# Layer 0 of a two-layer decoder trunk: one pair of K's columns in the place of V's second half behind the first projection, the input's statistics on two engines, V's second half behind the mixer's end

## The chip, the cores and the metric

The kernel runs on one core of a Trainium2 chip, as one program. The metric is the device time of one execution in microseconds (us), the median of the runs shown. The core has a tensor engine (PE) that writes matrix products into PSUM banks, a vector engine (DVE), a scalar engine (ACT), a third elementwise engine (POOL), and a queue engine (SP) that issues most transfers (DMA) between HBM and the core's memory SBUF.

## What is computed

Two post-norm layers over 512 tokens of width 1024, all in float32. The reference, cut to the parts that matter here:

```python
h = layer_norm(x, ln0_g, ln0_b)
for l in range(DEPTH):                      # DEPTH = 2
    mix = hybrid_mixer(h, w_in[l], ...)     # causal convolution (31 taps) + gated linear attention
    h = layer_norm(DEEPNORM_ALPHA * h + mix, ln1_g[l], ln1_b[l])
    xa = memory_cross_attention(h, mem, w_xq[l], w_xkv[l], w_xo[l])
    h = layer_norm(DEEPNORM_ALPHA * h + xa, ln2_g[l], ln2_b[l])
    ff = swiglu(h, w_ffn_in[l], w_ffn_out[l])
    h = layer_norm(DEEPNORM_ALPHA * h + ff, ln3_g[l], ln3_b[l])

def hybrid_mixer(h, w_in, ...):
    c_a, c_g, q, k, v, r, a_low = jnp.split(h @ w_in, cuts, axis=-1)
    u = causal_depthwise_conv(c_a * jax.nn.sigmoid(c_g), conv_w, conv_b)
    u = jax.nn.silu(layer_norm(u, conv_ln_g, conv_ln_b))
    ...
    o = rms_norm(gla_chunked(q, k, v, log_a), gla_norm_g) * jax.nn.silu(r)
    return jnp.concatenate([u, o], axis=-1) @ w_out

def memory_cross_attention(x, mem, w_q, w_kv, w_o):
    k, v = jnp.split(mem @ w_kv, 2, axis=-1)   # K and V need mem and weights only
    ...
```

K and V of the cross-attention (256 memory rows, 1024 columns each) depend on the memory and the weights alone. So their projections can stand anywhere ahead of the attention, and the kernel uses them as work for PE where PE would otherwise wait.

## The kernel before, in words

**Tiling.** Tokens lie in four tiles h0 to h3 of 128 rows. A projection is 128x128 weights against up to 512 moving columns. Each float32 operand is split into a high and a low part: ACT copies the high part (`hi`), DVE or POOL subtracts it from the source (`lo`), and `mm3` issues three matmuls (lines 170 to 172: high with high, high with low, low with high). A weight chunk of 512 KB comes through `wchunk`: a DMA by SP into one of 4 raw buffers, the high copy on ACT (line 161), the low part on the engine that `wlo_engines` named last (line 163), into one of 4 ring buffers. `split` (lines 111, 112) does the same to activations and evictions. The PSUM tag `acc` has four banks; `tr` and `cv` have two each.

**Order.** Each engine runs its own queue in order. The order is laid down when the program is built, by a scheduler that goes by estimated durations and priorities (`high_priority` brings forward, the convolution's taps have the lowest). `issue_after(x)` puts the instructions traced within it behind x, on x's engine alone.

**Front of layer 0.** `first_V` loads the memory, transposes it and computes V's first half (512 columns, 4 chunks, lines 163 to 172 on tiles pt_xv_first). Then the four x tiles are loaded. V's second half (pt_xv, again 4 chunks of weights, 48 matmuls of 512 columns) is worked between the steps of the first layer norm, and is written as a generator with pauses: first its first chunk, then after the statistics three of its parts, and its last part behind the transposes of k = 3. The statistics: `bn_stats` on DVE twice a tile (line 788) and `bn_aggr`, tile 3's behind the low part of V's first chunk; then a chain of ten small DVE instructions to y0 and b0 (lines 790 to 792); ACT normalises the four tiles (line 805); PE transposes 32 blocks (lt_ln, line 811); ACT scales each of eight k tiles (xf, line 813) and `split` makes hT. The first matmul of the mixer's projection (pp_c) needs hT's first tile and the first chunk of w_c.

**Mixer.** `conv_in` projects two halves to u, `conv_taps` runs 31 taps on each of four channel tiles on DVE (line 887, lowest priority), and gates, q, k, v and the state S of the linear attention (GLA) are worked beside them.

**Mixer's end, layer 0.** In the program's order: the first half of `conv_norm` (cn: transposes cvt, line 1009, statistics, chain to b at line 1015, evictions by ACT at line 1019); K's first pair of columns (`mem_K` with pr = 0: 256 columns, 2 chunks, 48 matmuls of 256 columns on pp_xk), its eviction behind that chain's end (end0); GLA's first pair with r's first group (pt_r), then r's second; the second half of cn (end1); K's pairs 1 to 3; the weights of the output projection (w_mo, 8 chunks, low parts behind end1); then the rest of cn and GLA's second pair. The output projection (po_mo) follows.

Of the kernel before, what the change touches and what calls it, by code (L numbers as in the profile page):

```python
# [51 lines left out]
def trunk(ctx: ExitStack, tc, a, out):  # L52
# [15 lines left out]
    def f(ap):  # L68
        return ap.bitcast(F32)
# [38 lines left out]


    def split(hi, lo, src, eng=DVE):  # L110
        ins = ACT.activation(hi, src, AF.Copy)  # L111
        eng.tensor_sub(lo, src, f(hi))  # L112
        return ins
# [19 lines left out]
    behind_act = []  # L133
    lo_end = [None]

# [33 lines left out]
    def mm3(o, lh, ll, rh, rl, start, stop):  # L169
        PE.matmul(o, lh, rh, start=start, stop=False)  # L170
        PE.matmul(o, lh, rl, start=False, stop=False)  # L171
        return PE.matmul(o, ll, rh, start=False, stop=stop)  # L172

# [78 lines left out]

    def proj_feat(w, mov, specs, name, n=T, halves=False, after=None):

        work = []
        for si, (c0, ncol, evac) in enumerate(specs):
            kk = 1024 // ncol
            wcs = [wchunk(w[ci * kk * P:(ci + 1) * kk * P, c0:c0 + ncol], kk, ncol, f"{name}{si}{ci}", after=after)
                   for ci in range(NK // kk)]
            banks = [bank(f"pp_{name}{si}{m}") for m in range(ncol // P)]  # L260
            work.append((kk, wcs, banks, evac))
        parts = [(0, n // 2), (n // 2, n)] if halves else [(0, n)]
        for t0, t1 in parts:
            for kk, wcs, banks, evac in work:
# [12 lines left out]

    def proj_tok(w, mov, c0, evac, name, groups=((0, 1), (2, 3)), after=None, pause=False):

        wcs = []

        def chunk(ci):
            wcs.append(wchunk(w[ci * 2 * P:(ci + 1) * 2 * P, c0:c0 + 512], 2, 512, f"{name}{ci}",
                              after=after if ci else None))

        for ci in range(1 if pause else 4):
            chunk(ci)
        if pause:  # L290
            yield
            for ci in (1, 2):
                chunk(ci)
        for grp in groups:
            banks = {tt: bank(f"pt_{name}_{tt}") for tt in grp}
            for ci in range(4):
                if pause and ci == 3:
                    yield
                    chunk(3)
                    yield  # L300
                wh, wl = wcs[ci]
# [391 lines left out]

    def mem_K(l, mT, KT, pr, after=None, evict_after=None):
# [4 lines left out]
        proj_feat(a["w_xkv"][l], mT, [(pr * 256, 256, evac)], f"xk{pr}_{l}", n=MEM, after=after)  # L699

    def new_V(l):
        return [block([P, 2, D], F32R, f"V{j}_{l}") for j in range(2)]

    def mem_V(l, mT, V, c, **kw):
        cs = slice(c * 512, (c + 1) * 512)
        return proj_tok(a["w_xkv"][l], mT, D + c * 512,
                     lambda mt, ps: split(V[0][:, mt, cs], V[1][:, mt, cs], ps), f"xv{c}_{l}", groups=((0, 1),), **kw)

# [11 lines left out]
    def first_V():  # L720
# [48 lines left out]
        return end, lo_end[0], evict  # L769

    V0_end, lo0_end, V0_evict = first_V()
    load_x(0, 1, 2, 3)
    nc.sync.dma_start(lnrow[0:NK, :], a["ln0_g"].rearrange("(k p) -> k p", p=P))
    nc.sync.dma_start(lnrow[NK:2 * NK, :], a["ln0_b"].rearrange("(k p) -> k p", p=P))
    KT = new_K(0)
    hT = new_hT("ln0")
    V1 = mem_V(0, mT, V, 1, pause=True)
    next(V1)
    V1_lo = lo_end[0]
    with tc.high_priority(offset=HP):  # L780
# [9 lines left out]
        DVE.tensor_scalar(v0, mv0[:, :, 1], EPS, VS, ALU.add, ALU.mult)  # L790
        y0 = rstd_of(v0, NT, "ln0")
        chain_end = DVE.scalar_tensor_tensor(b0, mv0[:, :, 0], -1.0, y0, ALU.mult, ALU.mult)
# [8 lines left out]
    with tc.issue_after(chain_end.ins):  # L801
        DVE.tensor_copy(lncol, pl[:, :2 * NK])
    with tc.high_priority(offset=HP):
        for tt in range(NT):
            normed = ACT.activation(h[tt], h[tt], AF.Identity, scale=y0[:, tt:tt + 1], bias=b0[:, tt:tt + 1])
        with tc.issue_after(normed.ins):
            next(V1)
        for k in range(NK):
            pt = bank(f"lt_ln0_{k}", tag=("tr", "cv")[k % 2])
            for tt in range(NT):  # L810
                turned = PE.transpose(pt[:, tt * P:(tt + 1) * P], h[tt][:, k * P:(k + 1) * P], ident)
            xf = tmp.tile([P, T], F32, tag="t", name=f"xf{k}")
            xf_ins = ACT.activation(xf, pt, AF.Identity, scale=lncol[:, k:k + 1], bias=lncol[:, NK + k:NK + k + 1])
# [21 lines left out]
    for l in range(L):  # L835
# [272 lines left out]
        if l > 0:  # L1108
# [156 lines left out]
```

## Time and profile before

| | |
|---|---|
| median of 3 runs | 1404.52 us (1404.28 to 1404.99) |
| profiled execution | 1405.92 us, span 1404.2 us |
| PE busy | 1379.3 us, 98% of the span |
| PE weight loads busy | 1235.1 us, 88% |
| DVE busy | 1076.7 us, 77% |
| ACT busy | 672.5 us, 48% |
| POOL busy | 160.3 us, 11% |
| HBM traffic | 163 GB/s over the span |

The span is one execution as the profiler saw it, the time adds what lies around it. An instruction's row gives its start, its duration, the engine, the line, what it writes and reads, and in brackets how long its engine had been idle and what ended that. Matmuls overlap: a row of 0.39 us can start every 0.23 us, so prices are taken from start to start. PEclk is the granted clock of PE as a share of full speed. "x" is a count of merged instructions.

### The profile page before, as it was taken

The page shows a single profiled execution, that of the slowest core. Times are in us where ns is not written, and L with a number is a line of the kernel's source. Part 1 is how long each engine was busy: PE and PEld are TensorE (multiplying, and loading weights), DVE is VectorE, ACT ScalarE, POOL GpSimd, SP SyncE. Part 2 cuts the span into 40 slices and gives each one's busy share as a digit, 9 for nine tenths or more (in the row PEclk, how much of TensorE's full clock was granted, in tenths as well). Part 3 has the DMA queues.
Part 4 walks back from the last instruction along what each step waited for, and adds up shares of the span by engine and source line. Part 5 has one row for each costly group of instructions (what it writes and reads, how often), then busy time and mean ns, then how long its engine had stood idle before and what let it go on. Part 6 is the DMA issues. An engine that isn't in the chain of part 4 may idle for free.

```text
span 1404.2 us, 22523 instructions
## 1 busy us (share of the span) xinstructions
PE 1379.3 (98%) x8847; PEld 1235.1 (88%) x8847; DVE 1076.7 (77%) x1901; ACT 672.5 (48%) x1108; POOL 160.3 (11%) x123
## 2 busy tenths in 40 slices
PE   8999799999999999999999999999999999999997
PEld 6788598988899899989897889889889998998996
DVE  6589885756888878877668999675569886878766
ACT  5663271343466456545345235624435653664551
POOL 0384001110000000001014200011100000000000
PEclk9999999999999999999999999999999999999998
DMA  6444166695255665565334234669814646646641
GB/s 250 147 131 138 32 193 168 197 270 163 76 135 150 195 176 144 167 191 135 122 99 161 64 116 166 232 156 264 204 61 123 179 143 190 178 136 200 160 136 60
DMA packets 131230, 217.95 MB, mean 155 GB/s; under 512 B 8988, under 2 KB 83440, under 8 KB 130612
## 3 DMA queue, kind: packets, MB, share of 16 engines
q1 hardware_dynamic: 118132, 176.40, 38.1%
q0 software_dynamic: 12704, 39.85, 14.7%
q8 instruction: 69, 1.13, 0.3%
q14 instruction: 37, 0.30, 0.1%
q10 hardware_dynamic: 288, 0.26, 0.1%
HBM read 191.32 MB, written 37.75 MB: 163 GB/s over the span
## 4 chain that ended last, share of the span: by engine, by line
PE 86%; DVE 8%; DMA 2%; ACT 2%; issue 1%; SPq 0%; DVEq 0%; ACTq 0%; POOLq 0%
PE fx L600 5%; PE fx L602 5%; PE fx L601 5%; DVE cv L887 4%; PE fw L602 3%; PE fw L601 3%; PE fw L600 3%; PE pp_xq L171 2%; PE pp_xq L170 2%; PE pp_xq L172 2%; PE po_xo L172 2%; PE po_xo L171 2%; PE po_xo L170 2%; PE po_mo L170 2%; PE po_mo L171 2%; PE po_mo L172 2%
## 5 line engine op out<-in xcount | busy, mean ns | idle before, releaser
L887 DVE SCALAR_TENSOR_TENSOR cv<-u,chan,cv 128x511 f32<-128x511 f32 (+29 forms) x240 | 159.8, 731 | 0.2
L112 DVE TENSOR_TENSOR w_s<-s,w_s 128x1024 fp32r<-128x1024 f32 x80 | 97.6, 1220 | 33.8 <-ACT w_s L111 33.3
L111 ACT ACTIVATE w_s<-s 128x1024 fp32r<-128x1024 f32 x80 | 84.4, 1056 | 63.6 <-DMA s<-raw_a 37.1
L355 POOL DMA_DIRECT2D s<-raw_a x40 | 34.8, 881 | 625.1 <-PE pp_f L172 142.6
L600 PE MATMUL fx<-T_ln,w_s 128*128 128x256 f32 x320 | 90.6, 284 | 0.0
L602 PE MATMUL fx<-T_ln,w_s 128*128 128x256 f32 x320 | 90.5, 283 | 0.0
L601 PE MATMUL fx<-T_ln,w_s 128*128 128x256 f32 x320 | 90.5, 283 | 0.0
L111 ACT ACTIVATE w_a<-raw_a 128x1024 fp32r<-128x1024 f32 x60 | 63.1, 1056 | 32.1 <-issue 10.5
L112 DVE TENSOR_TENSOR w_a<-raw_a,w_a 128x1024 fp32r<-128x1024 f32 x60 | 73.2, 1220 | 4.7 <-ACT w_a L111 4.3
L222 ACT ACTIVATE junk<-h,nm_ln 128x1024 uint8<-128x1024 f32 x18 | 20.7, 1150 | 103.3 <-DVE nm_ln L221 100.9
L600 PEld LDWEIGHTS fx<-T_ln,w_s 128*128 128x128 f32 x320 | 61.4, 192 | 0.3 <-ACT u L613 0.2
L601 PEld LDWEIGHTS fx<-T_ln,w_s 128*128 128x128 f32 x320 | 61.4, 192 | 0.0
L602 PEld LDWEIGHTS fx<-T_ln,w_s 128*128 128x128 f32 x320 | 61.4, 192 | 0.0
L171 PE MATMUL pp_xq<-hT_ln,w_xq 128*128 128x256 f32 (+1 forms) x192 | 61.0, 321 | 0.0
L170 PE MATMUL pp_xq<-hT_ln,w_xq 128*128 128x256 f32 (+1 forms) x192 | 60.2, 321 | 0.5 <-ACT hT_ln L111 0.5
L172 PE MATMUL pp_xq<-hT_ln,w_xq 128*128 128x256 f32 (+1 forms) x192 | 60.1, 319 | 0.0
L171 PE MATMUL pp_c<-hT_ln,w_c 128*128 128x512 f32 (+1 forms) x160 | 55.3, 348 | 0.2 <-DVE hT_ln L112 0.2
L172 PE MATMUL pp_c<-hT_ln,w_c 128*128 128x512 f32 (+1 forms) x160 | 55.2, 348 | 0.0
L170 PE MATMUL pp_c<-hT_ln,w_c 128*128 128x512 f32 (+1 forms) x160 | 53.9, 349 | 0.7 <-DVE h L344 0.5
L355 POOL DMA_DIRECT2D S_fs<-w_ffn_out x16 | 17.2, 1073 | 313.9 <-DMA S_fs<-w_ffn_out 252.2
L111 ACT ACTIVATE w_S_fo<-raw_S_fo 128x1024 fp32r<-128x1024 f32 x32 | 33.8, 1058 | 36.0 <-PE foX_fo L563 14.2
L171 PE MATMUL po_xo<-w_xo,oTh 128*128 128x512 f32 x128 | 49.8, 392 | 0.0
(399 smaller groups left out, 4858.1 us busy)
## 6 DMA issues: line engine op xcount, KB each, us to landing
raw_a<-w_ffn_in SPq DMA_DIRECT2D x60, 512.0 KB, 3.7
s<-raw_a POOLq DMA_DIRECT2D x40, 512.0 KB, 5.5
raw_fo<-w_ffn_out SPq DMA_DIRECT2D x36, 512.0 KB, 3.4
S_fs<-w_ffn_out SPq DMA_DIRECT2D x32, 512.0 KB, 7.5
raw_S_fo<-S_fs SPq DMA_DIRECT2D x32, 512.0 KB, 4.4
s<-w_ffn_in SPq DMA_DIRECT2D x20, 512.0 KB, 5.4
raw_c<-w_in SPq DMA_DIRECT2D x16, 512.0 KB, 4.8
raw_xk<-w_xkv SPq DMA_DIRECT2D x16, 512.0 KB, 3.5
```

Source lines behind the costliest of these rows:

```text
L111: ins = ACT.activation(hi, src, AF.Copy)
L112: eng.tensor_sub(lo, src, f(hi))
L170: PE.matmul(o, lh, rh, start=start, stop=False)
L171: PE.matmul(o, lh, rl, start=False, stop=False)
L172: return PE.matmul(o, ll, rh, start=False, stop=stop)
L222: ACT.activation(junk, ht, AF.Square, bias=nm, accum_out=v)
L355: POOL.dma_start(dst, src, accum_op=ALU.add, max_dma_last_dim=4096)
L600: PE.matmul(o, wh, bh, start=start and k == 0, stop=False, skip_group_check=True)
L601: PE.matmul(o, wh, bl, start=False, stop=False, skip_group_check=True)
L602: PE.matmul(o, wl, bh, start=False, stop=stop and k == 3, skip_group_check=True)
L887: DVE.scalar_tensor_tensor(cv[ct][:, s:], u[:, ct, :T - s], wj, cv[ct][:, s:], ALU.mult, ALU.add)
```

## The change

In the front, V's second half is gone; in its place the first pair of K's columns is worked, in two steps (its first chunk, and after the statistics' chain the rest). x's first tile is loaded ahead of V's last chunk, and its statistics go behind a memory split on DVE. Tile 1's statistics are made on ACT as two sums, tiles 2 and 3 on DVE behind the low part of V's last chunk; the low part of V's third chunk goes to POOL. K's first chunk is split behind the statistics of tile 3, and the chain behind that split. The transposes go behind K's last matmul. Tiles 1 and 3 are normalised on DVE, and xf of k = 3, 5 and 7 is made there. At the mixer's end K's pair 1 comes first and is evicted without a tie, r is finished before cn starts, and the order is then GLA's first pair, K's pair 2, cn's second half, K's pair 3, V's second half (its DVE work behind end1), w_mo. Layer 1 keeps its order.

```diff
 def first_V():
+        turned_lo = lo_end[0]
+        wlo_engines(POOL)
         chunk(2, copied)
+        wlo_engines(DVE)
         mem_load(1, 1)
+        load_x(0)
+        with tc.issue_after(turned_lo.ins):
+            stats(0)
         with tc.issue_after(turned.ins):
             turned, copied = turn_after(work(1, 0), 1, 1)
         chunk(3, copied)
...
+    def stats_act(tt):
+        with tc.high_priority(offset=HP):
+            sm = small.tile([P, 2], F32, tag="sums", name=f"sums_ln0{tt}")
+            nm = small.tile([P, 1], F32, tag="nm", name=f"nm_ln0{tt}")
+            ACT.activation(junk, h[tt], AF.Copy, accum_out=sm[:, 0:1])
+            DVE.tensor_scalar(nm, sm[:, 0:1], -1.0 / D, None, ALU.mult)
+            ACT.activation(junk, h[tt], AF.Square, bias=nm, accum_out=sm[:, 1:2])
+            DVE.tensor_scalar(mv0[:, tt, :], sm, 1.0 / D, None, ALU.mult)
...
-    load_x(0, 1, 2, 3)
+    load_x(1, 2, 3)
...
-    V1 = mem_V(0, mT, V, 1, pause=True)
-    next(V1)
-    V1_lo = lo_end[0]
+    stats_act(1)
+    with tc.issue_after(lo0_end.ins):
+        stats(2)
+        st3 = stats(3)
+    K0_pause = mem_K(0, mT, KT, 0, parts=True)
+    with tc.issue_after(st3.ins):
+        next(K0_pause)
+    first_lo = lo_end[0]
     with tc.high_priority(offset=HP):
-        for tt in range(NT):
...
+        with tc.issue_after(first_lo.ins):
+            DVE.tensor_scalar(v0, mv0[:, :, 1], EPS, VS, ALU.add, ALU.mult)
         y0 = rstd_of(v0, NT, "ln0")
         chain_end = DVE.scalar_tensor_tensor(b0, mv0[:, :, 0], -1.0, y0, ALU.mult, ALU.mult)
-    with tc.issue_after(chain_end.ins):
+    with tc.issue_after(chain_end.ins), tc.issue_after(V0_end.ins):
+        next(K0_pause)
+        run(K0_pause)
         V0_evict()
-    with tc.issue_after(chain_end.ins), tc.issue_after(V0_end.ins):
-        next(V1)
+    K0_end = mm_end[0]
...
-    with tc.high_priority(offset=HP):
+    with tc.high_priority(offset=HP), tc.issue_after(K0_end.ins):
         for tt in range(NT):
-            normed = ACT.activation(h[tt], h[tt], AF.Identity, scale=y0[:, tt:tt + 1], bias=b0[:, tt:tt + 1])
-        with tc.issue_after(normed.ins):
-            next(V1)
+            if tt % 2:
+                DVE.tensor_scalar(h[tt], h[tt], y0[:, tt:tt + 1], b0[:, tt:tt + 1], ALU.mult, ALU.add)
+            else:
+                ACT.activation(h[tt], h[tt], AF.Identity, scale=y0[:, tt:tt + 1], bias=b0[:, tt:tt + 1])
...
+            if k in (3, 5, 7):
+                DVE.tensor_scalar(xf, pt, g_, b_, ALU.mult, ALU.add)
+            else:
+                xf_ins = ACT.activation(xf, pt, AF.Identity, scale=g_, bias=b_)
             split(hT[0][k // 4][:, k % 4, :], hT[1][k // 4][:, k % 4, :], xf)
-            if k == 3:
-                with tc.issue_after(turned.ins), tc.issue_after(xf_ins.ins):
-                    run(V1)
...
 # the mixer's end, layer 0
-            with tc.high_priority(offset=HP):
-                end0, took0 = next(cn)
-            mem_K(l, mT, KT, 0, evict_after=end0)
+            mem_K(l, mT, KT, 1)
             gla = gla_pair(0)
             next(gla)
+            run(proj_r)
+            r_end = mm_end[0]
+            wlo_engines(DVE)
+            with tc.high_priority(offset=HP), tc.issue_after(r_end.ins):
+                end0, took0 = next(cn)
             with later(end0):
                 run(gla)
-            run(proj_r)
-            wlo_engines(DVE)
+            mem_K(l, mT, KT, 2)
             with tc.high_priority(offset=HP):
                 end1, took1 = next(cn)
-            for pr in range(1, 4):
-                mem_K(l, mT, KT, pr, after=end0 if pr > 1 else None, evict_after=end1 if pr > 1 else end0)
+            mem_K(l, mT, KT, 3, after=end0)
+            with later(end1):
+                mem_V(l, mT, V, 1)
```

More of the change, by code (lines that the diff above doesn't have):

```diff
@@ L133, in trunk @@
     behind_act = []
-    lo_end = [None]
     def behind(load):
@@ L171, in mm3 @@
         PE.matmul(o, lh, rl, start=False, stop=False)
-        return PE.matmul(o, ll, rh, start=False, stop=stop)
+        mm_end[0] = PE.matmul(o, ll, rh, start=False, stop=stop)
+        return mm_end[0]
     def rstd_of(v, n, name):
@@ L251, in layer_norm, with proj_feat, proj_feat_parts @@
             split(hT[0][i][:, :, ts_], hT[1][i][:, :, ts_], pv)
-    def proj_feat(w, mov, specs, name, n=T, halves=False, after=None):
+    def proj_feat(*args, **kw):
+        run(proj_feat_parts(*args, **kw))
+    def proj_feat_parts(w, mov, specs, name, n=T, halves=False, after=None, parts=False):
         work = []
@@ L257, in proj_feat @@
             kk = 1024 // ncol
-            wcs = [wchunk(w[ci * kk * P:(ci + 1) * kk * P, c0:c0 + ncol], kk, ncol, f"{name}{si}{ci}", after=after)
-                   for ci in range(NK // kk)]
+            wcs = []
+            for ci in range(NK // kk):
+                wcs.append(wchunk(w[ci * kk * P:(ci + 1) * kk * P, c0:c0 + ncol], kk, ncol, f"{name}{si}{ci}", after=after))
+                if parts:
+                    yield
             banks = [bank(f"pp_{name}{si}{m}") for m in range(ncol // P)]
             work.append((kk, wcs, banks, evac))
-        parts = [(0, n // 2), (n // 2, n)] if halves else [(0, n)]
-        for t0, t1 in parts:
+        for t0, t1 in [(0, n // 2), (n // 2, n)] if halves else [(0, n)]:
             for kk, wcs, banks, evac in work:
@@ L276, in proj_feat, with proj_tok @@
                             evac(m, bk[:, :n])
[L278 to L293, printed above, removed]
+    def proj_tok(w, mov, c0, evac, name, groups=((0, 1), (2, 3))):
+        wcs = [wchunk(w[ci * 2 * P:(ci + 1) * 2 * P, c0:c0 + 512], 2, 512, f"{name}{ci}") for ci in range(4)]
         for grp in groups:
             banks = {tt: bank(f"pt_{name}_{tt}") for tt in grp}
[L296 to L301, printed above, removed]
+            for ci, (wh, wl) in enumerate(wcs):
                 for tt in grp:
@@ L692, in later, with mem_K @@
         return tc.issue_after(ins.ins) if ins is not None else nullcontext()
-    def mem_K(l, mT, KT, pr, after=None, evict_after=None):
+    def mem_K(l, mT, KT, pr, after=None, evict_after=None, parts=False):
         def evac(m, ps):
@@ L697, in evac, with mem_V @@
                 split(KT[0][:, pr * 2 + m, :], KT[1][:, pr * 2 + m, :], ps)
-        proj_feat(a["w_xkv"][l], mT, [(pr * 256, 256, evac)], f"xk{pr}_{l}", n=MEM, after=after)
+        work = proj_feat_parts(a["w_xkv"][l], mT, [(pr * 256, 256, evac)], f"xk{pr}_{l}", n=MEM, after=after, parts=parts)
+        return work if parts else run(work)
     def new_V(l):
         return [block([P, 2, D], F32R, f"V{j}_{l}") for j in range(2)]
-    def mem_V(l, mT, V, c, **kw):
+    def mem_V(l, mT, V, c):
         cs = slice(c * 512, (c + 1) * 512)
-        return proj_tok(a["w_xkv"][l], mT, D + c * 512,
-                     lambda mt, ps: split(V[0][:, mt, cs], V[1][:, mt, cs], ps), f"xv{c}_{l}", groups=((0, 1),), **kw)
+        run(proj_tok(a["w_xkv"][l], mT, D + c * 512,
+                     lambda mt, ps: split(V[0][:, mt, cs], V[1][:, mt, cs], ps), f"xv{c}_{l}", groups=((0, 1),)))
     def load_x(*tts):
@@ L769, in first_V, with stats @@
         return end, lo_end[0], evict
+    mv0 = const.tile([P, NT, 2], F32, name="mv0")
+    v0 = const.tile([P, NT], F32, name="v0")
+    b0 = const.tile([P, NT], F32, name="b0")
+    def stats(tt):
+        with tc.high_priority(offset=HP):
+            st = ln_stats(tt, "ln0")
+            for i in range(2):
+                end = DVE.bn_stats(st[:, i, :], h[tt][:, i * 512:(i + 1) * 512])
+            DVE.bn_aggr(mv0[:, tt, :], st)
+        return end
+    def stats_act(tt):
+        with tc.high_priority(offset=HP):
+            sm = small.tile([P, 2], F32, tag="sums", name=f"sums_ln0{tt}")
[4 more added lines that the diff above has]
+            DVE.tensor_scalar(mv0[:, tt, :], sm, 1.0 / D, None, ALU.mult)
     V0_end, lo0_end, V0_evict = first_V()
-    load_x(0, 1, 2, 3)
+    load_x(1, 2, 3)
     nc.sync.dma_start(lnrow[0:NK, :], a["ln0_g"].rearrange("(k p) -> k p", p=P))
@@ L1115, in trunk @@
             for c in range(2):
-                run(mem_V(l, mT, V, c))
+                mem_V(l, mT, V, c)
             mo = []
```

16 lines of the change are left out of this document (4 added, 12 removed).

## The prediction

> **What bounds the kernel now.** I read the busy table of the page, then what the tensor engine (PE) waited for, then stretches around those waits, then the order in time there.
>
> ```profile
> span 1404.2 us, 22523 instructions
> ...
> PE 1379.3 (98%) x8847; PEld 1235.1 (88%) x8847; DVE 1076.7 (77%) x1901; ACT 672.5 (48%) x1108; POOL 160.3 (11%) x123
> ```
>
> ```profile
> PE pt_r L170 <- DVE KT L112: 3.8, 1, 3.8
> PE cvt L1009 <- ACT acc L889: 3.2, 2, 1.8
> PE lt_ln L811 <- ACT h L805: 1.7, 1, 1.7
> ...
> PE po L1065 <- DVE attT L1055: 1.3, 1, 1.3
> PE pt_xv L171 <- DVE w_xv L163: 1.0, 2, 0.5
> ```
>
> PE is the bound, so only PE time that is idle or at a slow clock can be won. The large waits stand at two places of layer 0: the front (lt_ln, pt_xv) and the mixer's end (pt_r, cvt, po).
>
> ```profile
> core 0: us, PE busy (x) PEld busy (x) DVE busy (x) ACT busy (x) POOL busy (x), PEclk, DMA share, GB/s
> 20.50:40.75 20.25, 17.25 (x83) 13.51 (x82) 12.99 (x26) 15.29 (x20) 0.00 (x0) 0.92 0.45 137
> 25.40:31.60 6.20, 4.04 (x12) 3.03 (x13) 4.55 (x9) 5.58 (x5) 0.00 (x0) 0.73 0.36 102
> 61.50:162.80 101.30, 98.02 (x550) 79.44 (x548) 96.47 (x158) 40.18 (x62) 56.98 (x24) 1.00 0.34 110
> 150.00:172.00 22.00, 13.77 (x106) 10.61 (x105) 19.50 (x54) 8.10 (x25) 0.00 (x0) 0.84 0.00 0
> 168.50:171.30 2.80, 2.78 (x7) 2.20 (x8) 2.41 (x13) 1.55 (x4) 0.00 (x0) 0.50 0.00 0
> 172.00:207.00 35.00, 35.00 (x298) 31.91 (x297) 25.92 (x47) 25.65 (x50) 0.00 (x0) 1.00 0.51 163
> ```
>
> Mixer's end, 150 to 172 us: 22.00 - 13.77 = 8.2 us idle, and 2.78 us of matmuls at clock 0.50, which lose 1.4 more: **9.6 us**. VectorE (DVE) is nearly full from 61.5 to 162.8 us (96.5 of 101.3): it runs the convolution's taps, and PE runs out of work before they end.
>
> ```profile
> 159.14 1.08 PE L1075 MATMUL po<-S,qk 64*64 64x128 f32 x12
> ...
> 159.32 3.50 DVE L887 SCALAR_TENSOR_TENSOR cv<-u,chan,cv 128x485 f32<-128x485 f32 x5
> ...
> 163.97 0.77 PE L1009 MATMUL cvt<-ident,acc 128*128 128x128 f32 x5 [1.39 <-ACT acc L889]
> ...
> 167.86 0.16 DVE L1015 SCALAR_TENSOR_TENSOR b<-mv,y_cln 128x2 f32<-128x2 f32 x1
> ...
> 168.52 0.80 PE L170 MATMUL pt_r<-w_r,hT_ln 128*128 128x512 f32 x1 [3.78 <-DVE KT L112]
> ...
> 175.07 1.03 PE L1009 MATMUL cvt<-ident,acc 128*128 128x128 f32 x8
> ...
> 182.50 0.39 PE L172 MATMUL pt_r<-w_r,hT_ln 128*128 128x512 f32 x1
> ...
> 183.75 0.16 DVE L1015 SCALAR_TENSOR_TENSOR b<-mv,y_cln 128x2 f32<-128x2 f32 x1
> ...
> 206.93 0.40 PE L170 MATMUL po_mo<-w_mo,cUh 128*128 128x512 f32 x1
> ```
>
> PE has used up its work at 160.2, the taps end at 162.8, and r's second half (pt_r) starts only at 168.5, because its PSUM banks are held by the first K columns, whose eviction is tied behind the first normalisation (b, 167.86).
>
> **The change part by part.** *Moves on PE.* Prices by start to start:
>
> ```profile
> 127.69 0.39 PE L171 MATMUL pt_v<-w_v,hT_ln 128*128 128x512 f32 x1
> ...
> 133.36 0.39 PE L172 MATMUL pt_v<-w_v,hT_ln 128*128 128x512 f32 x1
> ...
> 134.71 0.39 PE L170 MATMUL pp_xk<-mT,w_xk 128*128 128x256 f32 x1
> ...
> 140.57 0.40 PE L170 MATMUL pt_r<-w_r,hT_ln 128*128 128x512 f32 x1
> ```
>
> 5.67 us for 25 steps of 512 columns is 0.227 each; 5.86 us for 48 of 256 columns is 0.122 each. V's second half is 48 of the first, 10.9 us; one K pair 48 of the second, 5.9 us. The front loses 5.0 us of work, the mixer's end gains the same: in sum nothing. What counts is the idle time.
>
> *Front before.* From 20.50 to 40.75 PE has 10.9 us of V, and 32 transposes at 0.11 (eight took 1.03), 3.5 us; with 0.2 for the small one, 14.6 of 20.25. **5.6 us** are lost.
>
> *Front after.* What ends last before the transposes is the statistics, then the chain to b, then the normalised tiles:
>
> ```profile
> 19.97 1.06 ACT L161 ACTIVATE w_xv<-raw_xv 128x1024 fp32r<-128x1024 f32 x1 [4.62 <-DMA raw_xv<-w_xkv]
> ...
> 23.76 0.17 DVE L790 TENSOR_SCALAR v<-mv 128x4 f32<-128x4 f32 x1
> ...
> 25.55 0.16 DVE L792 SCALAR_TENSOR_TENSOR b<-mv,y_ln 128x4 f32<-128x4 f32 x1
> 25.75 4.64 ACT L805 ACTIVATE h<-h,b,y_ln 128x1024 f32<-128x1024 f32 x4 [1.86 <-DVE b L792]
> ...
> 40.75 0.71 PE L170 MATMUL pp_c<-hT_ln,w_c 128*128 128x512 f32 x2
> ```
>
> ```profile
> L163 DVE TENSOR_TENSOR w_xk<-raw_xk,w_xk 128x1024 fp32r<-128x1024 f32 x14 | 17.0, 1220 | 0.7 <-ACT w_xk L161 0.6
> ...
> L187 DVE TENSOR_SCALAR t_ln<-y_ln,v_ln 128x1 f32<-128x1 f32 x48 | 13.0, 271 | 1.0
> ...
> L1186 DVE TENSOR_SCALAR p<-p,ss 128x256 f32<-128x256 f32 x32 | 10.1, 357 | 0.5
> ...
> L193 DVE TENSOR_SCALAR y_ln<-t_ln,y_ln 128x1 f32<-128x1 f32 x24 | 5.1, 212 | 0.6
> ...
> L885 DVE TENSOR_SCALAR cv<-u,chan 128x512 f32<-128x512 f32 x8 | 6.4, 810 | 0.1
> ```
>
> The first weight chunk still comes by DMA at about 19.9: in SP's queue the same loads stand before it, with x's first tile moved ahead of V's last chunk. Its split takes 1.06 on ACT and 1.22 on DVE, to 22.2, and the chain (23.76 to 25.71, 2.0 us) now follows at once, since tiles 2 and 3 had their statistics before it and tile 1 on ACT, which waited 4.62 us there. The chain ends at 24.2, 1.5 us earlier. That DVE tile 0's statistics wait for x, and that V's third chunk is split on POOL at 2.4 instead of 1.2 us, I cost at nothing: V's first half is not what ends last; without that cover it would be some 1.2 us.
>
> Normalising: two tiles on ACT (2.3 us) beside two on DVE. DVE's price bounds from rows: 128x512 into PSUM took 810 ns, 539 above the two-scalar 128x1 form, so 1.05 ns an element and 1.35 us for 1024; 128x256 within SBUF took 357, 145 above the one-scalar form, 0.57 ns an element and 0.85 us. The h tiles lie in SBUF like the second, so I take 0.85; either way ACT's 2.3 us hides most of it. All four tiles are ready near 26.5 (before: 30.4). The Trainium skill (VectorE: DVE Perf Modes, Mode 2×_2P) says that a one-source fp32 operation wholly in SBUF runs at two elements a cycle; the two rows agree (0.57 against 1.05 ns), and by a rate of one a cycle the sum would be 0.5 us less won, 1397.5.
>
> K's second chunk is split behind the chain. Behind two tiles on DVE's queue it ends at 24.2 + 1.7 + 1.2 = 27.1, ahead of them at 25.4; eight matmuls wait for it, and behind K's last one stand all transposes. I take the later, some 28, for the first transpose. First projection matmul at about 30, not 40.75. By then PE has done 5.9 of K and 16 transposes (1.8) of 9.5: 1.8 us lost. From there ACT and DVE make hT:
>
> ```profile
> L813 ACT ACTIVATE xf<-lt_ln,lncol 128x512 f32<-128x512 f32 x8 | 6.0, 789 | 2.6 <-PE lt_ln L811 2.6
> L111 ACT ACTIVATE hT_ln<-xf 128x512 fp32r<-128x512 f32 x8 | 4.9, 648 | 0.0
> ```
>
> ACT: five xf and eight hi copies at some 0.7, and three weight splits of 1.06: 12 us to 41. DVE: eight lo at 0.69, three xf at 0.81, three to four weight splits, V's eviction 1.3: as much. One k tile each 1.5 us; PE needs 1.4 us for g's two banks on it, plus the transposes, so it about keeps pace; I add 1.3 us of starving, from nothing (PE paced by g, then a) to 4 (a's weights late). The clock: after a wait of 1.7 us and sparse work it was 0.73 over 25.40 to 31.60; I put 1.0 for that (0 to 1.7). Lost after: 1.8 + 1.3 + 1.0 = 4.1, **1.5 us won** (bounds: 2.5 lost, 4.5 won). The Trainium skill (TensorE: Matmul & The Clock Gate, Part 1) ties the half clock to an idle window of about 3.4 us. By it the short gaps would cost no clock, the front would win 2.5, and the time would be 1396.0; this trace shows 0.73 after a wait of 1.7 us, so I keep my 1.0.
>
> *Transfers.* SP issues two chunks of 512 KB instead of four in the front (the two weight chunks and x in order, so the projection's first chunk comes no later than before, nearer 22 than 32, if a raw buffer is free); at the mixer's end it issues four of V ahead of w_mo's eight, two of K fewer. There the DMA engines were busy at 0.51, 163 GB/s; 1 MB more is 6 us of that rate beside 35 us, and V's tie on DVE comes later than its data: nothing, unless the four raw buffers hold w_mo's loads behind V's splits (in the 8.4 below).
>
> *Mixer's end after.* K's second pair is evicted at once, so r's second half has banks and runs on: 10.9 us of work from the point where PE stood. It covers the 2.6 us to the taps' end, and PE reaches r's end some 8 us after it. K's eviction takes 0.8 us of DVE from the taps, covered by those 8. The normalisation's transposes are tied behind r; from their start (163.97) to b took 4.0 us, and K's third pair (5.9) hides it. Second round: before, 175.07 to 183.75 is 8.8 us, the chain's steps interleaved with weight splits on DVE's in-order queue. In that time PE has K's fourth pair (5.9, its low halves behind the first b) and V's half (10.9, low halves behind the second b, two thirds of its matmuls need only high halves). From r's end PE then has 5.9 + 5.9 + 10.9, and transposes and GLA: 24.2 before from 182.7 to 206.9, less three K pairs, 6.6, and two rounds of transposes and GLA's (2.7) that stood earlier; 32 us in all. DVE's additional work here is four V splits (4.9) and V's eviction (1.3), less two K splits (2.4) and one K eviction (0.8), which come earlier: 3.0 us, against 9.1 idle in 172 to 207; ACT adds four V splits and an eviction less the same of K, 2.5 us, against 9.4. It fits, but narrowly between the second b and w_mo, where DVE's queue is in order and w_mo's splits stand behind V's. I keep the 1.3 us of attT and take 2.2 us of new waits (0 to 8.4: PE through with the third pair 7.6 us after r's end, and the fourth pair's splits only behind a second b at 16). Lost after 3.5, **6.1 us won** (0 to 9.6).
>
> Sum: 7.6 us. The profiled execution took 1405.92 us (span 1404.2, 1.7 around it), 1.4 above the median of 1404.52; from that median the sum gives **1397.0 us**.
>
> **Rivals.** *Both places fill better:* no new wait at the end, front wins 3: 9.6 + 3.0 - 1.3 = 11.3, 1393. For it: hT can start 10 us earlier. Against: DVE and ACT are then both full in 30 to 41. *The hole moves:* r's second half is free, but PE then waits for the first b and splits, six or so of the 9.6 us return, front nothing: 3 us won, 1401.5. For it: the chain now starts after r, not after the taps. *DVE takes over the end (slower):* from the second b to w_mo DVE has to do K and V splits (7.3), four of w_mo (4.9), evictions (2.1), GLA's part and the convolution's low halves (11): 25 us; if b comes 16 us after r's end and DVE waits for ACT as in 172 to 207, w_mo starts 46 us after r's end instead of 32, 14 us lost for the 9.6, the front's 1.5 besides: 1407.4. It decides once DVE is more than 11 us late.
>
> **How the numbers follow.** Forecast (1394.5 to 1400) 0.55; fills better 0.20; hole moves (1400 to 1404) 0.14, of which 0.05 is faster by over 0.2% (2.8 us, about what a measurement of this kernel can tell from no change) and 0.09 within; slower rival 0.11, of which 0.02 within. Faster 0.80, same 0.11, slower 0.09. The range leaves out the slower rival, the edge of the hole and a quarter of the better case: 1391.5 to 1403.0; the forecast's own is 1394.5 to 1400.
>
> **What would show it.** Right: pt_r no longer waits for KT and its matmuls run gapless; the first pp_c near 30; b of the input near 24.2; no clock of 0.50 at 168 to 171. Wrong: waits of pt_xv or pp_xk on DVE splits above 3 us, po_mo on w_mo, or pp_c on hT above 3.

## The result and the profile after

| | before | changed |
|---|---|---|
| median | 1404.76 us (4 runs, 1404.28 to 1407.18) | 1397.73 us (4 runs, 1396.80 to 1399.64) |
| profiled execution, its span | 1405.92, 1404.2 | 1397.67, 1396.0 |
| first matmul of the gates (al) | 63.20 | 56.85 |
| first matmul of the output projection (po_mo) | 206.93 | 198.21 |
| from al to po_mo | 143.7 | 141.4 |

The changed kernel takes 0.9948 of the time before (95% interval 0.9931 to 0.9966), about 7 us less. The forecast was 1397.0.

Two milestones split the gain. al comes 6.35 us earlier, of which 5.0 (at the prediction's prices) is work that moved to the mixer's end: 1.35 won in the front. From al to po_mo it takes 2.4 us less (143.73 against 141.36) with those 5.0 us more to do: 7.4 won at the mixer's end. The rest of the program, from po_mo on, took 1197.3 us before and 1197.8 now; over all traces here this stretch lies between 1196.7 and 1202.8, so differences of a few us between single whole runs say little, and the reasons below are read from the two milestones.

The page of the changed kernel, its busy table:

```profile
span 1396.0 us, 22513 instructions
...
PE 1376.8 (99%) x8847; PEld 1233.4 (88%) x8847; DVE 1078.4 (77%) x1904; ACT 671.7 (48%) x1107; POOL 162.8 (12%) x124
```

What PE waited for, by engine, line and releaser (sum, times, longest):

```profile
PE pa L1068 <- DVE cOl L1117: 1.4, 1, 1.4
PE pp_c L171 <- ACT hT_ln L113: 1.1, 2, 0.8
PE lt_ln L829 <- ACT xf L835: 0.7, 2, 0.5
PE cvb L1044 <- ACT csl L1046: 0.6, 1, 0.6
PE pt_xv_first L172 <- POOL w_xv_first L164: 0.5, 1, 0.5
...
PE cvb L1044 <- ACT acc L1037: 0.4, 1, 0.4
```

The four large waits of before (pt_r on KT, cvt on acc, lt_ln on h, po on attT) are all gone. In their place stand small ones, and one of them, pt_xv_first on POOL, is new in the front. (In GLA, attT holds the masked scores, pa their matmuls and po the output; gr is r as ACT evicts it. cvt and cvb are the convolution's transposes ahead of its normalisation and behind it.) The stretches that were shown before, now:

```profile
core 0: us, PE busy (x) PEld busy (x) DVE busy (x) ACT busy (x) POOL busy (x), PEclk, DMA share, GB/s
20.50:40.75 20.25, 18.43 (x114) 15.02 (x112) 18.18 (x34) 16.91 (x26) 0.00 (x0) 1.00 0.50 140
150.00:172.00 22.00, 22.00 (x165) 20.02 (x164) 17.27 (x41) 13.17 (x32) 0.00 (x0) 1.00 0.27 94
172.00:207.00 35.00, 32.46 (x221) 27.03 (x221) 29.68 (x64) 22.00 (x44) 1.22 (x1) 1.00 0.67 220
```

150 to 172 us is full at full clock, where 8.2 us were idle. From 172 to 207 PE now idles 2.5 us, where it did not before. The rows behind it, in order of time:

```profile
21.08 0.39 PE L173 MATMUL pt_xv_first<-w_xv_first,mT 128*128 128x512 f32 x1
...
23.86 0.16 DVE L808 SCALAR_TENSOR_TENSOR b<-mv,y_ln 128x4 f32<-128x4 f32 x1
23.94 1.23 DVE L164 TENSOR_TENSOR w_xk<-raw_xk,w_xk 128x1024 fp32r<-128x1024 f32 x1
...
25.70 1.34 DVE L823 TENSOR_SCALAR h<-h,y_ln,b 128x1024 f32<-128x1024 f32 x2
...
27.72 1.91 PE L829 MATMUL lt_ln<-ident,h 128*128 128x128 f32 x16
29.34 1.45 ACT L835 ACTIVATE xf<-lt_ln,lncol 128x512 f32<-128x512 f32 x2
...
30.68 1.06 ACT L162 ACTIVATE w_c<-raw_c 128x1024 fp32r<-128x1024 f32 x1
31.62 0.78 ACT L835 ACTIVATE xf<-lt_ln,lncol 128x512 f32<-128x512 f32 x1
32.29 1.06 ACT L162 ACTIVATE w_c<-raw_c 128x1024 fp32r<-128x1024 f32 x1
33.24 1.67 ACT L113 ACTIVATE hT_ln<-xf 128x512 fp32r<-128x512 f32 x3
33.92 1.20 PE L171 MATMUL pp_c<-hT_ln,w_c 128*128 128x512 f32 x4 [0.81 <-ACT hT_ln L113]
...
147.04 0.60 ACT L1054 ACTIVATE gr<-pt_r 128x512 f32<-128x512 f32 x1 [9.99 <-PE pt_r L173]
...
161.92 0.39 PE L173 MATMUL pt_r<-w_r,hT_ln 128*128 128x512 f32 x1
162.15 1.03 PE L1027 MATMUL cvt<-ident,acc 128*128 128x128 f32 x8
166.11 0.16 DVE L1033 SCALAR_TENSOR_TENSOR b<-mv,y_cln 128x2 f32<-128x2 f32 x1
...
178.21 0.15 DVE L1033 SCALAR_TENSOR_TENSOR b<-mv,y_cln 128x2 f32<-128x2 f32 x1
178.28 4.63 DVE L164 TENSOR_TENSOR w_xv<-raw_xv,w_xv 128x1024 fp32r<-128x1024 f32 x4
178.35 0.68 PE L1068 MATMUL pa<-qk 64*64 64x64 f32 x16 [1.45 <-DVE cOl L1117]
...
198.21 0.39 PE L171 MATMUL po_mo<-w_mo,cUh 128*128 128x512 f32 x1
```

The reader is to see three things. The chain's b and the transposes stand where they were forecast, but the first pp_c stands 4 us later than forecast; two weight splits of ACT (30.68, 32.29) stand ahead of the first copies to hT (33.24). At the mixer's end ACT evicts r's first group (gr) at 147.04; in the kernel before it did so only at 165.23:

```profile
165.23 1.08 ACT L1036 ACTIVATE gr<-pt_r 128x512 f32<-128x512 f32 x2
```

And the second normalisation's b is ready 16.2 us after r's end (178.36 against 162.15), which is the point that the rival "DVE takes over" named.

### The profile page after: what moved, and what is told of

It reads as the page before. It is cut to its first block, busy times and chain, and to the rows that moved or that the text cites. A ratio compares the mean times of both kernels' runs of the same rounds, so it can differ in the third digit from the quotient of the medians.

```text
span 1396.0 us, 22513 instructions
## 1 busy us (share of the span) xinstructions
PE 1376.8 (99%) x8847; PEld 1233.4 (88%) x8847; DVE 1078.4 (77%) x1904; ACT 671.7 (48%) x1107; POOL 162.8 (12%) x124
## 4 chain that ended last, share of the span: by engine, by line
PE 93%; DVE 3%; DMA 2%; ACT 2%; issue 1%; POOL 0%; SPq 0%; DVEq 0%; ACTq 0%; POOLq 0%
PE fx L591 5%; PE fx L593 5%; PE fx L592 5%; PE fw L591 3%; PE fw L593 3%; PE fw L592 3%; PE pp_xq L172 2%; PE pp_xq L171 2%; PE pp_c L172 2%; PE pp_xq L173 2%; PE pp_c L173 2%; PE po_mo L171 2%; PE po_mo L172 2%; PE po_mo L173 2%; PE po_xo L172 2%; PE po_xo L171 2%
## 5 line engine op out<-in xcount | busy, mean ns | idle before, releaser
L591 PEld LDWEIGHTS fx<-T_ln,w_s 128*128 128x128 f32 x320 | 61.4, 192 | 0.5 <-ACT u L604 0.5
L592 PEld LDWEIGHTS fx<-T_ln,w_s 128*128 128x128 f32 x320 | 61.4, 192 | 0.0
L593 PEld LDWEIGHTS fx<-T_ln,w_s 128*128 128x128 f32 x320 | 61.4, 192 | 0.0
L113 ACT ACTIVATE w_S_fo<-raw_S_fo 128x1024 fp32r<-128x1024 f32 x32 | 33.8, 1058 | 36.0 <-PE foX_fo L554 14.2
```

The lines of the kernel that those rows point to most:

```text
L591: PE.matmul(o, wh, bh, start=start and k == 0, stop=False, skip_group_check=True)
L592: PE.matmul(o, wh, bl, start=False, stop=False, skip_group_check=True)
L593: PE.matmul(o, wl, bh, start=False, stop=stop and k == 3, skip_group_check=True)
```

## The experiments

All ratios are to the kernel before. The milestones are from each run's trace; "V to al" runs from the start of the last matmul of V's first half (pt_xv_first) to al.

| kernel | front | V to al | al to po_mo | time | ratio (95%) |
|---|---|---|---|---|---|
| before | old | 43.0 | 143.7 | 1404.76 | 1 |
| changed | new | 35.8 | 141.4 | 1397.73 | 0.9948 (0.9931 to 0.9966) |
| e1_before_untied | old | 41.3 | 133.6 | 1396.32 | 0.9934 (0.9919 to 0.9949) |
| e2_oldfront_newend | old | 41.3 | 137.3 | 1400.03 | 0.9963 (0.9949 to 0.9977) |
| e3_newfront_oldend | new | 35.7 | 140.4 | 1398.02 | 0.9945 (0.9930 to 0.9960) |
| e4_V_untied | new | 35.5 | 138.6 | 1395.23 | 0.9930 (0.9913 to 0.9947) |
| e5_stats_dve | new | 36.1 | 140.9 | 1399.37 | 0.9953 (0.9939 to 0.9966) |
| e6_norm_act | new | 38.2 | 140.6 | 1401.77 | 0.9968 (0.9956 to 0.9981) |
| e7_lo_dve | new | 36.4 | 141.0 | 1399.99 | 0.9951 (0.9937 to 0.9966) |
| e8_hold_hi | new | 33.9 | 141.1 | 1396.01 | 0.9922 (0.9907 to 0.9938) |
| e9_newfront_e1order | new | 35.7 | 137.8 | 1394.69 | 0.9914 (0.9899 to 0.9929) |
| e10_gr_late | new | 35.7 | 146.3 | 1403.93 | 0.9983 (0.9973 to 0.9993) |
| e11_untied_hold | new | 33.9 | 137.8 | 1393.33 | 0.9908 (0.9895 to 0.9922) |
| e12_neworder_V_hold | new | 33.8 | 138.6 | 1395.43 | 0.9923 (0.9910 to 0.9937) |

The changed kernel was timed beside runs of the kernel before with a median of 1404.76, and the others in three groups (e1 to e4; e6 to e9; e5 and e10 to e12) beside runs with medians of 1405.1, 1407.0 and 1406.0, so ratios are compared across groups, and times within one. With the new front 5.0 us of al to po_mo is work that the old one does earlier. Each milestone is from one trace. How far they repeat is seen where nothing differs: kernels with the changed kernel's front have V to al within 0.3 us (35.5 to 35.8), those with its mixer's end have al to po_mo within 0.8 us (140.6 to 141.4).

**What made the hole at the mixer's end.** e1 is the kernel before with one tie removed.

```diff
-            mem_K(l, mT, KT, 0, evict_after=end0)
+            mem_K(l, mT, KT, 0)
```

> The kernel before, with one edit: the eviction of K's first pair at the mixer's end is not tied behind the first normalisation. Theory A (the hole at the mixer's end is PSUM banks held by that eviction): r's second half gets its banks at once, the wait of pt_r on KT (3.8 us) goes, PE idle between 150 and 172 us falls from 8.2 to 3 us or less, no clock of 0.50 follows, and the time falls by 5 to 7 us to about 1398 to 1400. Theory B (the convolution's chain sets the end, whatever PE does before it): r is done earlier, the same time is lost behind it, and the time is 1403 or more.

One word less in the old kernel is worth 10.1 us from al to po_mo, at least as much as the whole change. Its waits from 140 to 212 us and its stretch from 150 to 172:

```profile
PE po L1065 <- DVE attT L1055: 0.8, 1, 0.8
```

```profile
150.00:172.00 22.00, 22.00 (x172) 19.14 (x169) 19.43 (x39) 12.11 (x31) 0.00 (x0) 1.00 0.15 48
```

e3 keeps the new front and puts the old order back, its tie too, with V's second half behind end1.

> The changed kernel's front, the old order at the mixer's end: first normalisation not behind r, K's pair evicted behind it, V's half behind K's last pair. Theory A: al at 56.9 as in the changed kernel, but the wait of pt_r on KT is back at 3 to 4 us, PE idle in the hole 7 us or more, time 1403 to 1405. Theory C (more work at the end fills it, in whatever order): no hole over 3 us, time 1397 to 1400.

The hole did not come back: no wait of pt_r, only one of 1.3 us for attT. The K eviction did stay tied (its low part ran at 166.9), but ACT evicted r's first group at 147.5, and r's second group, from 152.19 on, can only have taken those banks:

```profile
147.53 0.60 ACT L1054 ACTIVATE gr<-pt_r 128x512 f32<-128x512 f32 x1 [9.98 <-PE pt_r L173]
```

So the tie alone does not make the hole. More than that: of the change's edits at the mixer's end e3 has only the move of V's half, and it is as fast as the changed kernel (0.9945 against 0.9948, al to po_mo 140.4 against 141.4). By these numbers Theory C held; its reason is tried next. e10 is e3 with r's evictions put back to where they stood on ACT in the kernel before, behind the convolution's copies.

```diff
-                    ACT.activation(accs[ct // 2][:, ct % 2, :], cv[ct], AF.Copy)
+                    acc_ins[0] = ACT.activation(accs[ct // 2][:, ct % 2, :], cv[ct], AF.Copy)
...
-            ACT.activation(gr[:, tt, :], ps, AF.Silu)
+            with tc.issue_after(acc_ins[0].ins) if l == 0 else nullcontext(): ACT.activation(gr[:, tt, :], ps, AF.Silu)
```

> The new front with the old order and the tie at the mixer's end (1398.0 when ACT evicted r's first group at 147.5, with no wait of r's second group), but r's evictions are put on ACT behind the convolution's copies, where they stood in the kernel before. Theory A (the hole needs both: the K eviction tied behind the first normalisation, and r's first group evicted late, so that r's second group has no banks): pt_r waits for KT again by 3 us or more, the clock of 0.50 or the like comes back around 165 to 172, from al to the output projection 146 to 149 us instead of 140.4 (the kernel before took 143.7 without V's 5.0 us), time 1403 to 1407. Theory B (r's place on ACT does not matter, V's second half behind the end is what fills the hole): 140 to 143, time 1398 to 1400.

The hole is back with the same work in it: 5.9 us more from al to po_mo than e3, and the time in the range of Theory A. That rules out that V's half alone had filled it (Theory B, and e3's Theory C). Its waits, a stretch and rows:

```profile
PE cvt L1027 <- ACT acc L907: 3.2, 2, 1.8
PE po L1083 <- DVE attT L1073: 1.2, 1, 1.2
PE pt_r L171 <- ACT gr L1054: 0.6, 1, 0.6
```

```profile
150.00:172.00 22.00, 18.22 (x102) 14.81 (x101) 17.75 (x50) 11.50 (x29) 0.00 (x0) 0.84 0.07 22
```

```profile
155.61 0.55 PE L1027 MATMUL cvt<-ident,acc 128*128 128x128 f32 x3 [1.81 <-ACT acc L907]
...
156.91 0.59 ACT L907 ACTIVATE acc<-cv 128x512 f32<-128x512 f32 x1
157.51 1.28 ACT L1054 ACT_TABLE_LOAD   x1
157.55 1.33 PE L1027 MATMUL cvt<-ident,acc 128*128 128x128 f32 x5 [1.39 <-ACT acc L907]
...
158.81 1.09 ACT L1054 ACTIVATE gr<-pt_r 128x512 f32<-128x512 f32 x2
...
159.46 0.80 PE L171 MATMUL pt_r<-w_r,hT_ln 128*128 128x512 f32 x1 [0.58 <-ACT gr L1054]
160.05 0.63 PE L172 MATMUL pt_r<-w_r,hT_ln 128*128 128x512 f32 x1
...
163.42 0.40 PE L171 MATMUL pt_r<-w_r,hT_ln 128*128 128x512 f32 x1
```

Theory A had the wait wrong: pt_r waits for gr by 0.6 us, not for KT by 3. But those 0.6 us are not the price of the late gr. On ACT gr stands behind the taps' last copy (156.91) and a table load of 1.28 us (in e3 that load ran at 136.26, while ACT was idle), so the banks of r's second group come free only at about 159.4. PE had run out of other work at about 153.8, and the two waits of cvt, which stands ahead of pt_r in PE's in-order queue, cover most of the time until then. PE is idle for 3.8 us in all, and the nine matmuls after it (159.46 to 163.42) run 0.44 us apart instead of 0.23, 1.9 us more.

The tie on KT comes on top. Counted from al, gr is evicted at the same point in the kernel before and in e10 (102.0 us), but pt_r starts at 105.3 in the one, on KT, and at 102.7 in the other, on gr. That is some 2.6 us, and al to po_mo differs by 2.4 (143.7 against 146.3 - 5.0 = 141.3). These shares do not say what each cure alone would win. Early banks of either kind should be enough for r's second group: e3 has gr's with the tie kept. In e1 both came early, since without the tie the scheduler also had gr evicted at 151.74, ahead of the convolution's copies, and r's second group runs on around cvt's first transposes (160.47). No run has the tie off and gr late.

**What the order behind r is worth.** e2 has the old front and the new order, with K's four pairs and no V at the end.

```diff
-            with tc.high_priority(offset=HP):
-                end0, took0 = next(cn)
-            mem_K(l, mT, KT, 0, evict_after=end0)
+            mem_K(l, mT, KT, 0)
             gla = gla_pair(0)
             next(gla)
+            run(proj_r)
+            r_end = mm_end[0]
+            wlo_engines(DVE)
+            with tc.high_priority(offset=HP), tc.issue_after(r_end.ins):
+                end0, took0 = next(cn)
             with later(end0):
                 run(gla)
-            run(proj_r)
-            wlo_engines(DVE)
+            mem_K(l, mT, KT, 1)
             with tc.high_priority(offset=HP):
                 end1, took1 = next(cn)
...
+            mem_K(l, mT, KT, 2, after=end0)
+            with later(end1):
+                mem_K(l, mT, KT, 3)
```

> The front of before (V's second half there, statistics on DVE), the new order at the mixer's end with K's four pairs and no V: K0, GLA's first pair, r, first normalisation behind r, K1, second normalisation, K2, K3 with its DVE work behind the second. Theory A: the order and the free banks are what was won at the end, so the first al matmul stays at 63.2 us, the output projection starts 5 to 7 us earlier than before's 206.9, and the time is 1398 to 1400. Theory C (V's 5.0 us of additional work is needed as a filler behind r): PE waits 3 to 5 us more behind r's end than in the changed kernel, output projection not before 204, time 1402 or more.

Nearer Theory A: po_mo comes at 198.71 without V's half as a filler, and the time is at the edge of A's range. But al did not stay at 63.2; it came at 61.40 (more on that below). e2 wins 6.4 us of al to po_mo, 3.7 less than e1. The reading here, which no run isolates, is that with r finished first PE has less to do while the two normalisations run one after the other: pa, po_mo and cvb wait 2.9 us together. e4 is the changed kernel with V's second half freed of end1.

```diff
-            with later(end1):
-                mem_V(l, mT, V, 1)
+            mem_V(l, mT, V, 1)
```

> The changed kernel, but V's half at the mixer's end has no tie behind the second normalisation. Theory A (its low halves stand on DVE too late, so that PE's queue waits 1.4 us for GLA's transposes and 0.4 for cvb with V's matmuls behind them): the waits at 177 to 179.5 us shrink to under 0.7, output projection 1 to 1.5 us before 198.2, time 1396 to 1397. Rival (the four splits of 1.22 us then stand ahead of the normalisation's chain on DVE's in-order queue): its second b comes 2 to 5 us later than 178.2, and the time is the same or up to 2 us longer.

Both theories had a part right: al to po_mo is 2.8 us shorter, though the second b comes 3.0 us later, counted from al (182.93 - 58.55 against 178.21 - 56.85): V's matmuls fill the wait for it, and one wait of 1.3 us (cvb on csl) is left. e9 takes the new front, the old order, and both of these ties off, the one on K's first pair there and the one on V.

```diff
             with tc.high_priority(offset=HP):
                 end0, took0 = next(cn)
-            mem_K(l, mT, KT, 1, evict_after=end0)
+            mem_K(l, mT, KT, 1)
...
-            with later(end1):
-                mem_V(l, mT, V, 1)
+            mem_V(l, mT, V, 1)
```

(This diff is against e3.)

> The changed kernel's front with the old order at the mixer's end, but with the first K eviction there (pair 1) not tied behind the first normalisation and V's second half not tied either. Theory A (the tie was the whole hole at the mixer's end, the order behind r is worth nothing or less): from al to the output projection 138 to 139.5 us, as with the new order and V untied (138.6); time 1394.5 to 1396.5, the same as the old kernel with that one tie removed (1396.3), since the new front is worth 0 to 0.5. Theory B (new front and removed tie add up, the front being worth the predicted 1.5): 1394.0 to 1395.0. Theory C (V's second half is a worse filler in the old order, since its low parts stand on DVE ahead of the second normalisation's chain): the chain to the second b later than 184, al to po_mo 140 or more, time 1397 to 1399.

Theory C is out: no wait of PE is listed from 140 to 212 us, and al to po_mo takes 137.8, 0.8 less than with the new order (e4). So the order behind r is worth nothing, as Theory A had it. The time, 1394.69, lies in the ranges of A and of B and does not tell them apart. That the tie was the whole hole, Theory A's other half, had e3 against it, and e10, run later, too.

**What the front is worth, and what limits it.** e6 normalises and scales on ACT alone.

```diff
-            if tt % 2:
+            if tt > NT:
...
-            if k in (3, 5, 7):
+            if k > NK:
```

> The changed kernel, but all four input tiles are normalised on ACT and all eight xf made there, as in the kernel before. Measured from the start of the last matmul of V's first half to the gates' first matmul (al): 35.7 us in the changed kernel. Theory A (ACT's queue sets the front: the first hT high copies stood at 33.2, behind xf and weight splits): two more tiles (2.3 us) and three more xf (2.4 us) on ACT delay al by 2 to 5 us, time +2 to +5 against the changed kernel (1399.5 to 1402.5). Theory B (K's matmuls and their splits set the transposes, DVE's queue the rest): less DVE work, ACT's extra hidden: al within 0.7 us, time 1397 to 1398.5.

Theory A: al comes 2.4 us later, counted from V. ACT's 4.64 us for four tiles end at 29.0, and the waits of lt_ln for xf grow from 0.7 to 3.2 us. ACT's queue is what limits the front behind the chain. e7 keeps the third V chunk's low part on DVE.

```diff
-        wlo_engines(POOL)
         chunk(2, copied)
-        wlo_engines(DVE)
```

> The changed kernel, but the low part of V's third weight chunk stays on DVE instead of POOL. Theory A (the POOL split of 2.4 us ends V's first half later, 0.9 us in the changed kernel's trace): the wait of pt_xv_first on POOL (0.5 us) is gone, V's first half ends 0.5 to 0.9 us earlier, al earlier by as much, time 1396.8 to 1397.3. Theory B (DVE then reaches the statistics 1.2 us later, the chain to b ends at 25.2 instead of 24.0, and K's second chunk with it): V ends earlier but al does not, time unchanged at 1397.7 or up to 1 us later.

The wait for POOL is gone, but V's last chunks now wait 0.5 us for DVE and 0.5 for ACT. V's last matmul starts at 20.51, where the kernels with POOL's split have it anywhere from 20.48 to 21.65 (23.01 in e4, whose first 21 us ran at clock 0.92). al stands at 56.93 against 56.85 in the changed kernel: Theory B's result, though not by its reason, since b ended at 24.07 here, too; K's own last matmul (27.65) holds the transposes. e5 makes tile 1's statistics on DVE.

```diff
-    stats_act(1)
     with tc.issue_after(lo0_end.ins):
+        stats(1)
         stats(2)
```

> The changed kernel, but tile 1's statistics are made on DVE instead of ACT: 1.29 us and a bn_aggr more on DVE ahead of K's first low part, two small ones less. Theory A (DVE's queue sets the chain): b at 25.2 instead of 24.0, K's second low part as much later, the transposes at 28.5 instead of 27.7, al 0.7 to 1.2 us later from V's last matmul (36.4 to 36.9 instead of 35.8), time 1398.3 to 1399.0. Theory B (the chain still ends ahead of K's last matmul, which sets the transposes, as when POOL's split was moved to DVE): al unchanged within 0.3, time 1397.7.

Theory B: b ends at 24.03 in place of 24.02, the transposes start at 27.72 in both, and al stands at 56.84 against 56.85 (V to al is 0.3 us longer because V ended earlier). In the changed kernel DVE stood idle for 0.75 us ahead of K's first low part, waiting for ACT's high part; here that wait is gone, so most of tile 1's statistics fit there. e8 changes what ACT does first.

```diff
-            split(hT[0][k // 4][:, k % 4, :], hT[1][k // 4][:, k % 4, :], xf)
+            hi_ins = split(hT[0][k // 4][:, k % 4, :], hT[1][k // 4][:, k % 4, :], xf)
...
-                behind_act += [None, xf_ins, xf_ins, xf_ins]
+                behind_act += [None, hi_ins, hi_ins, hi_ins]
```

> The changed kernel, but the high copies of w_c's chunks are held on ACT behind the second k tile's high copy, not behind its xf, so that ACT makes the first two hT high copies ahead of the weight splits. In the changed kernel the first projection matmul (pp_c) started at 33.9, of which two weight splits of 1.06 us stood ahead of the first high copy. Theory A (that order on ACT is what starves the first projection): pp_c starts 1 to 2 us earlier, al 0.5 to 1.5 us earlier (34.2 to 35.2 from V's last matmul instead of 35.7), time 1396.2 to 1397.2. Theory B (ACT's whole work from 24 to 41 us is what counts, not its order): the first matmul waits for w_c's high part instead, al unchanged within 0.3 us, time 1397.7.

Theory A, and by al more than it expected. ACT's rows, and PE's first projection matmul:

```profile
28.72 2.11 ACT L835 ACTIVATE xf<-lt_ln,lncol 128x512 f32<-128x512 f32 x3
30.72 1.15 ACT L113 ACTIVATE hT_ln<-xf 128x512 fp32r<-128x512 f32 x2
31.76 2.00 ACT L162 ACTIVATE w_c<-raw_c 128x1024 fp32r<-128x1024 f32 x2
```

```profile
31.74 0.71 PE L171 MATMUL pp_c<-hT_ln,w_c 128*128 128x512 f32 x2
```

The same instructions in another order: hT's first copies 2.5 us earlier, pp_c 2.2 (0.6 of both because V ended earlier in this run), and V to al 1.9 us shorter.

**The best of both.** e11 is e9 with e8's edit, e12 is e4 with it.

> Changed front with hT's first two high copies ahead of the weight splits on ACT, old order at the mixer's end with pair 1's eviction and V's half untied. Theory A (the two gains add): V's last matmul to al 33.9, al to the output projection 137.8, time 1391 to 1393. Theory B (an earlier al only makes the mixer wait longer for the convolution's taps on DVE, which set its end): al to the output projection 139.5 or more, time 1394 to 1395.

> The same front, with the changed kernel's order at the mixer's end and only V's second half untied. Theory A (the order behind r is worth nothing beside the untied eviction): time within 1 us of the one with the old order, 1391.5 to 1393.5. Theory B (finishing r ahead of the normalisation leaves PE short behind r, pa and cvb waiting 2 us): al to the output projection 139 to 140, time 1393.5 to 1395.

The gains add in the trace (33.9 and 137.8), and the time is 0.3 us above Theory A's range. e11 is the fastest kernel here, 1393.33 us, 0.9908 (0.9895 to 0.9922) of before; that interval lies below the changed kernel's. No wait of PE is listed from 140 to 212 us in it. With the changed order (e12) al to po_mo is again 0.8 us longer, and the time 2.1 us, of which 1.1 lie behind po_mo; neither theory's ranges hold that (138.6 and 1395.43).

## Why the prediction was right, point by point

The forecast held in time and sign. Of its mechanisms, the chain, the transposes and the gapless pt_r came as it said, and the clock of 0.50 is gone. By po_mo the traces give 8.7 us won (206.93 - 198.21) for its sum of 7.6, by the medians 7.0. (1404.52 - 7.6 is 1396.9; the prediction wrote 1397.0.) Part of that is luck: the front's balance rests on a stall of the one profile it started from, and the mixer's end did not need the step on which the prediction rested.

- **Front, 1.5 won; by al 1.35.** The balance is right, its parts are not. From the last V matmul to the first pp_c the kernel before took 20.5 us and the changed one 12.8. Less that matmul (0.2) and the work at the prediction's prices (14.6 and 9.6), that is 5.7 and 3.0 lost: 2.7 won. From pp_c to al it takes 0.5 us more (22.9 against 22.4), and V's first half ends 0.84 us later. And 1.7 of the old front's 5.7 are its slow clock, which it does not always have (below).
- **First pp_c near 30: wrong, 33.92.** The 2 us from the first transpose to pp_c were too few: it took 6.2. The step "one k tile each 1.5 us" counted ACT's work but not its order: two weight splits stood ahead of the first copies to hT. e8, without them there, has pp_c at 31.74, still 1.7 late. Nor did the sum hold ACT's copies of V's and K's evictions (1.08, 0.38 and 0.40 us), which stood on ACT ahead of the first xf, at 29.34.
- **V's third chunk on POOL, costed at nothing:** PE waits 0.5 us for it in every run that has it. The 0.84 us by which V's first half ended later arise mostly there: the matmul behind that wait starts at 16.18, its like in the kernel before at 15.47. The memory's arrival, for which PE waited 0 to 1.3 us from run to run, differs little between these two traces (0.15 and 0.22). Taking POOL out (e7) put other waits in its place and brought al no earlier.
- **The clock, 1.0 lost after: nothing was lost,** and the old front loses it only sometimes: in e1 and e2, with the same old front, it stayed at full clock and al came at 61.5 and 61.4 instead of 63.20. Against those the new front does not win by al: 61.5 - 56.85 - 5.0 = -0.35. So the 1.35 that agrees with the forecast's 1.5 is luck. With the first tie off on both sides (e9 against e1) al wins 61.54 - 56.34 - 5.0 = 0.2, and po_mo comes 1.0 us earlier, 0.8 of it behind al, which is as much as kernels with the same mixer's end differ by. A front worth about 1 us at most is all that these runs support, and the ratios, 0.9914 and 0.9934, have intervals that overlap.
- **The chain's end 24.2: 24.02.** Its reason was half wrong: statistics on ACT did not bring it (e5). The transposes at 28: 27.72. Normalising on DVE: two tiles in 1.34 us, 0.67 each instead of 0.85. The Trainium skill (VectorE: DVE Perf Modes, Mode 2×_2P) has a one-source fp32 operation within SBUF run at two elements a cycle; this row agrees, being 0.65 ns an element with all that is fixed, against 1.05 for the row from PSUM.
- **Mixer's end, 6.1 won; measured 7.4.** pt_r runs gapless to 161.92 and cvt follows it. The new waits were put at 2.2 and measured 1.4 + 0.6 + 0.4 = 2.4. The 1.3 us of attT, which was kept, vanished. The hole itself was put down to the tie on K's eviction alone. In the old kernel the removal of that tie does win it back (e1). But the hole needs a late eviction of r's first group as well: with the tie kept, e3 has no hole and takes the changed kernel's time, and putting only that eviction back costs 5.9 us (e10). In the changed kernel the scheduler placed it early, which the prediction did not foresee.
- **The rivals.** "The hole moves" did not happen: K's third pair hid the first normalisation (162.15 to 166.27, 4.1 us). "DVE takes over" had its point right, the second b at 16.2 us after r's end, but not its price: po_mo started 36.1 us after r's end instead of 46. Until that b PE had K's third and fourth pairs (162.94 to 175.28), and K's splits (2.35 us at 166.26) were done. From b to po_mo DVE was busy 16.3 of 19.8 us, where the rival counted 25 us of work, and most of V's matmuls filled PE then. "Both fill better" (1393) is what e11 reaches, with another order on ACT, the old order at the mixer's end and the tie on V off.

## What to carry to other kernels

When a tensor engine waits for a PSUM bank, list everything that decides when that bank is free: the tie in the code, but also the other banks of the pool and the place of their evictions on their engine's queue. The wait that the trace names can be small because other waits stand ahead of it (0.6 us of a hole of 5.7 in e10). Here one tie less (e1) moved both evictions and gave as much as a change in two stages. Where an engine is the limit of a short stage, its order counts beside its sum: two weight splits ahead of two copies cost 1.9 us (e8). And a stall seen in one profile, such as the slow clock of the old front, should be looked for in a second one before a gain is built on it.

## What the runs showed of the hardware

The same waits do not always cost the clock. The kernel before ran at 0.73 from 25.40 to 31.60 us; e1, with the same front and the same waits (1.7 us for h, twice 0.5 for w_xv), did not:

```profile
25.40:31.60 6.20, 4.13 (x20) 3.28 (x21) 4.54 (x9) 5.59 (x5) 0.00 (x0) 1.00 0.36 104
```

e2 was at 1.00 there too. The Trainium skill (TensorE: Matmul & The Clock Gate, Part 1) calls the window by which the clock is set free-running and says that the point of the transition depends on where in it the first matmul lands; that the same front was slow in one trace of three would fit such a phase, but no run shows the phase. Its condition of an idle window of some 3.4 us does not fit so well: the slow stretch of the kernel before followed a wait of 1.7 us, and e10's slow matmuls (from 159.46 on) followed waits of 1.81, 1.39 and 0.58 with transposes between them. ACT's table load ahead of gr (ACT_TABLE_LOAD in the rows) is another cost that depends on its place: it takes 1.28 us, in the way at 157.51 in e10 and hidden at 136.26 in e3.
